# Fifteen small loads of 15 down to 1 partitions behind the first chunk of a softmax kernel

## The chip, the core and the metric

The kernel runs on one core of one Trainium2 chip. The metric is the device time of one execution in microseconds (us); less is better. A program on one core shows no second, slower state in these runs: all of them were of state fast, at a granted clock of 1.00. Each comparison was made on one chip, with runs of the kernel before in between.

## The reference

A softmax over the last axis of a float32 tensor of 16 x 256 x 32768, with temperature 1:

```python
scaled = logits / temperature
scaled = scaled - scaled.max(axis=-1, keepdims=True)
exp_scaled = np.exp(scaled)
return exp_scaled / exp_scaled.sum(axis=-1, keepdims=True)
```

It reads 536.87 MB and writes 536.87 MB. There is one exponential per element; the traffic to and from HBM (431 GB/s over the span of the kernel before) sets the scale, as the profile below shows.

## The kernel before

Each row of 32768 numbers is cut into two halves of 16384, which lie on two partitions. So there are 64 groups of 128 partitions, each of two chunks of 128 x 8192 numbers (4 MB, 32 KB a partition). A chunk is loaded into one of six buffers, worked on in place, and stored from the same buffer. VectorE takes the maximum, ScalarE the exponential; after both chunks of a group a few small instructions give the factor, and the two engines scale half of a chunk each. All loads and stores are issued from one queue, SyncE's, in program order:

```python
_BUFS = 6
_LAST_DMA = 4096

def load(i):                       # chunk i
    g, c = divmod(i, C)
    xs = xpool.tile([P, CW], fp32, tag="x", name="xs")
    slots[i] = xs
    for s, n in spans(CW, _LAST_DMA if g in (0, G - 1) else CW):   # first group: two halves
        tc.keep_in_program_order(
            nc.sync.dma_start(out=xs[:, s : s + n],
                              in_=x[g * P : (g + 1) * P, c * CW + s : c * CW + s + n]))

# ... store(), exps(), factors(), scales() cut ...

order = [("L", i) for i in range(min(_BUFS, n_chunks))] + [("S", 0)]
for i in range(1, n_chunks):
    order.append(("S", i))
    if i + _BUFS - 1 < n_chunks:
        order.append(("L", i + _BUFS - 1))
```

Six chunks are loaded at the start, as eight transfers, because the two chunks of the first group go in halves. From there on a store and a load alternate. In the text, 0a and 0b are the two halves of chunk 0, 1a and 1b those of chunk 1, L2 is the load of chunk 2, S0 the store of chunk 0.

## Time and profile before

| | before |
|---|---|
| median (lowest to highest) | 2494.44 us (2492.15 to 2495.24, 6 runs) |
| share of the chain of waits that is DMA | 96% |
| busy VectorE, ScalarE | 60%, 56% |
| rate from 500 to 2400 us | 433 GB/s |

These lines are from the page of the kernel before: the slices of the span (DMA is the mean busy share of the 16 DMA engines in tenths, GB/s what they moved), and the chain of work that ended last.

```profile
DMA  9999999999999999999999999999999999999998
GB/s 412 433 430 432 429 431 432 433 433 434 433 434 432 435 432 435 432 435 431 436 431 435 432 434 433 434 433 433 433 433 433 433 433 434 434 433 434 432 431 368
...
DMA 96%; SPq 1%; ACT 1%; DVE 1%; issue 1%; ACTq 0%
```

The DMA engines are busy for 90% or more of every slice but the last, and 96% of the chain runs through them. The rate is 433 GB/s from 500 us to 2400 us. Against that, only the first slice (412) and the last (368) leave something.

The next view is the table of stages: for each window, its length, the busy time of VectorE, ScalarE and GpSimd with their instruction counts, the clock, the mean busy share of the DMA engines and the rate in GB/s.

```profile
core 0: us, DVE busy (x) ACT busy (x) POOL busy (x), PEclk, DMA share, GB/s
6.00:12.00 6.00, 0.00 (x0) 0.00 (x0) 0.00 (x0) 1.00 1.01 434
12.00:18.00 6.00, 5.11 (x1) 1.28 (x1) 0.00 (x0) 1.00 1.02 437
18.00:24.00 6.00, 4.90 (x2) 2.39 (x1) 0.00 (x0) 1.00 1.02 437
...
125.00:500.00 375.00, 223.21 (x145) 210.89 (x69) 0.00 (x0) 1.00 1.00 431
500.00:2400.00 1900.00, 1138.55 (x735) 1072.70 (x344) 0.00 (x0) 1.00 1.00 433
2440.00:2500.00 60.00, 14.66 (x17) 15.47 (x9) 0.00 (x0) 1.00 0.74 318
```

From 6 us on the engines work without a break (DMA share 1.00 to 1.02) until the last 60 us. The rate is 2 GB/s lower up to 500 us than later.

The queue's own timeline shows how the opening loads are issued (start, length, what; consecutive issues are merged; SPq is SyncE's queue, L64 a line of the kernel), and VectorE's shows when the first two halves of the first group are there:

```profile
0.73 3.92 SPq L64 DMA_DIRECT2D xs<-in_logits_dram  x8
```

```profile
12.89 8.69 DVE L107 TENSOR_REDUCE nm<-xs 128x1 f32<-128x8192 f32 x1 [12.89 <-DMA xs<-in_logits_dram]
22.68 8.69 DVE L107 TENSOR_REDUCE nm<-xs 128x1 f32<-128x8192 f32 x1 [1.10 <-DMA xs<-in_logits_dram]
```

All eight opening loads are issued by 4.65 us, without a wait, so some 58 us of work lie before the DMA engines (the last of these loads landed at 62.21 us).

**Out of step, counted from the trace.** Two counts are in the trace but on no page.

The first is the spread of landing marks. Each transfer over 128 partitions left 16 marks on its semaphore, one by one: the first half of chunk 0, for one, from 7.55 to 7.93 us. There are 16 DMA engines, so the author takes each mark for the end of one engine's share, and the time from the first to the last of the 16 for how far apart the engines are; the trace does not name the engines. Before, it is 0.35 us for the opening loads, 0.60 us at 100 us, 2.0 at 200, 4.2 at 300, 6.5 at 500, then 7.1 at 1000, 8.5 at 1500, and 10.45 us for the last store. So, read this way, the engines do get out of step without help.

The second is the excess of long packets. Most packets of one 32 KB row took 1.213 us, those of a 16 KB row 0.611 us. What longer packets took beyond that is, summed over the 16 engines, 23.2 us up to 62 us, 2.5 us from 62 to 120 us, 26.8 us from 120 to 500 us, and 7.6 us in all the time after.

### The profile page before, as it was taken

The page shows a single profiled execution, that of the slowest core. Times are in us where ns is not written, and L with a number is a line of the kernel's source. Part 1 is how long each engine was busy: PE and PEld are TensorE (multiplying, and loading weights), DVE is VectorE, ACT ScalarE, POOL GpSimd, SP SyncE. Part 2 cuts the span into 40 slices and gives each one's busy share as a digit, 9 for nine tenths or more (in the row PEclk, how much of TensorE's full clock was granted, in tenths as well). Part 3 has the DMA queues.
Part 4 walks back from the last instruction along what each step waited for, and adds up shares of the span by engine and source line. Part 5 has one row for each costly group of instructions (what it writes and reads, how often), then busy time and mean ns, then how long its engine had stood idle before and what let it go on. Part 6 is the DMA issues. An engine that isn't in the chain of part 4 may idle for free.

```text
span 2493.8 us, 2234 instructions
## 1 busy us (share of the span) xinstructions
DVE 1487.4 (60%) x964; ACT 1405.0 (56%) x455; POOL 0.2 (0%) x4
## 2 busy tenths in 40 slices
DVE  7655565556655566555665566655666566655663
ACT  5665554655556555565555655555546555465553
POOL 0000000000000000000000000000000000000000
DMA  9999999999999999999999999999999999999998
GB/s 412 433 430 432 429 431 432 433 433 434 433 434 432 435 432 435 432 435 431 436 431 435 432 434 433 434 433 433 433 433 433 433 433 434 434 433 434 432 431 368
DMA packets 37745, 1073.90 MB, mean 431 GB/s; under 512 B 4192, under 2 KB 4192, under 8 KB 4192
## 3 DMA queue, kind: packets, MB, share of 16 engines
q1 hardware_dynamic: 37728, 1073.76, 99.9%
q14 instruction: 17, 0.14, 0.0%
HBM read 536.87 MB, written 536.87 MB: 431 GB/s over the span
## 4 chain that ended last, share of the span: by engine, by line
DMA 96%; SPq 1%; ACT 1%; DVE 1%; issue 1%; ACTq 0%
DMA out_dram<-xs 93%; DMA xs<-in_logits_dram 2%; SPq L64 1%; DVE nm L107 1%; ACT xs L163 1%; ACT xs L114 0%; ACTq L224 0%; SPq L75 0%; DVE f L150 0%; ACT ee L131 0%; DVE rS L149 0%; DVE Sh L87 0%; DVE ttj L138 0%; DVE Sh L84 0%; DVE Sh L138 0%
## 5 line engine op out<-in xcount | busy, mean ns | idle before, releaser
L114 ACT ACTIVATE xs<-xs,nm 128x8192 f32<-128x8192 f32 (+1 forms) x130 | 912.1, 7016 | 972.4 <-DVE nm L107 972.4
L107 DVE TENSOR_REDUCE nm<-xs 128x1 f32<-128x8192 f32 (+1 forms) x130 | 1111.6, 8551 | 527.3 <-DMA xs<-in_logits_dram 527.3
L163 ACT ACTIVATE xs<-xs,f 128x4096 f32<-128x4096 f32 (+1 forms) x130 | 468.1, 3648 | 71.4 <-DVE f L150 71.4
L160 DVE TENSOR_SCALAR xs<-xs,f 128x4096 f32<-128x4096 f32 (+1 forms) x130 | 295.7, 2318 | 3.7 <-DVE f L150 1.8
L138 DVE CUSTOM_DVE_ANT_0 ttj<-ee,ssum 128x2 f32<-128x2 f32 x64 | 10.3, 161 | 423.8 <-ACT ee L131 423.8
L114 ACT ACTIVATION_READ_ACCUMULATOR xs<-xs,nm 128x1 f32 x130 | 24.2, 186 | 0.0
L131 ACT ACTIVATE ee<-nm,nMh 128x2 f32<-128x2 f32 x64 | 17.9, 280 | 0.0
L150 DVE TENSOR_SCALAR f<-ee,rS 128x2 f32<-128x2 f32 x64 | 14.6, 229 | 2.2
L149 DVE RECIPROCAL rS<-Sh 128x1 f32<-128x1 f32 x64 | 10.5, 164 | 2.2
L87 DVE TENSOR_TENSOR nMh<-nMh 128x1 f32<-128x1 f32 x64 | 10.2, 160 | 2.2
L87 DVE TENSOR_TENSOR Sh<-Sh 128x1 f32<-128x1 f32 x64 | 10.2, 160 | 2.2
L129 DVE TENSOR_REDUCE nMh<-nm 128x1 f32<-128x2 f32 x64 | 9.9, 155 | 2.2
L84 DVE STREAM_SHUFFLE nMh<-nMh 128x1 f32<-128x1 f32 x64 | 9.7, 151 | 0.0
L84 DVE STREAM_SHUFFLE Sh<-Sh 128x1 f32<-128x1 f32 x64 | 9.7, 151 | 0.0
L114 ACT ACT_TABLE_LOAD x1 | 1.3, 1283 | 12.9 <-DMA xs<-in_logits_dram 12.9
L138 DVE DVE_READ_ACCUMULATOR2_ANT Sh<- 128x1 f32 x64 | 5.3, 84 | 0.0
L84 DVE LOAD_MASK_SELECT Sh<-Sh x64 | 0.9, 14 | 2.8
L84 DVE LOAD_MASK_SELECT nMh<-nMh x64 | 0.9, 14 | 2.7
L210 POOL MEMSET const-bfloat16-1.0<- 128x1 bf16 x1 | 0.1, 102 | 0.0
L210 POOL MEMSET const-uint8-127<- 128x1 uint8 x1 | 0.1, 102 | 0.0
L210 POOL MEMSET const-float32-0.0<- 128x1 f32 x1 | 0.1, 99 | 0.2 <-issue 0.2
L210 POOL MEMSET const-float32-1.0<- 128x1 f32 x1 | 0.1, 99 | 0.0
## 6 DMA issues: line engine op xcount, KB each, us to landing
out_dram<-xs SPq DMA_DIRECT2D x126, 4096.0 KB, 38.2
xs<-in_logits_dram SPq DMA_DIRECT2D x124, 4096.0 KB, 29.0
xs<-in_logits_dram SPq DMA_DIRECT2D x8, 2048.0 KB, 22.3
out_dram<-xs SPq DMA_DIRECT2D x4, 2048.0 KB, 26.7
```

Source lines behind the costliest of these rows:

```text
L64: nc.sync.dma_start(out=xs[:, s : s + n], in_=x[g * P : (g + 1) * P, c * CW + s : c * CW + s + n],)
L84: nc.vector.stream_shuffle(out=v[:, j + 1 : j + 2], in_=v[:, j : j + 1], mask=mask)
L87: nc.vector.tensor_tensor(out=v[:, j + 1 : j + 2], in0=v[:, j : j + 1], in1=v[:, j + 1 : j + 2], op=op,)
L107: nc.vector.tensor_reduce(out=nm[:, k : k + 1], in_=xs[:, s : s + n], axis=X, op=A.max, negate=True)
L114: nc.scalar.activation(out=xs[:, s : s + n], in_=xs[:, s : s + n], func=Exp, bias=nm[:, k : k + 1], scale=inv_t, accum_out=ssum[:, k : k + 1],
L129: nc.vector.tensor_reduce(out=nMh[:, 0:1], in_=nm, axis=X, op=A.min)
L131: nc.scalar.activation(out=ee, in_=nm, func=Exp, bias=nMh[:, n_rounds : n_rounds + 1], scale=-1.0,)
L138: nc.vector.tensor_tensor_reduce(out=ttj, in0=ee, in1=ssum, scale=1.0, scalar=0.0, op0=A.mult, op1=A.add, accum_out=Sh[:, 0:1],)
L149: nc.vector.reciprocal(out=rS, in_=Sh[:, n_rounds : n_rounds + 1])
L150: nc.vector.tensor_scalar_mul(out=f, in0=ee, scalar1=rS)
L160: nc.vector.tensor_scalar_mul(out=xs[:, s : s + cut], in0=xs[:, s : s + cut], scalar1=f[:, k : k + 1])
L163: nc.scalar.activation(out=xs[:, s + cut : s + n], in_=xs[:, s + cut : s + n], func=Copy, scale=f[:, k : k + 1],)
```

## The change

The intent: loads of 15, 14, ..., 1 partitions should give each engine one more small packet than the next, so that all engines are out of step from the start and the long packets are spared. The data go to the buffer of chunk 5, which is loaded over them later.

```diff
+_STAGGER = 512
@@ load
-        xs = xpool.tile([P, CW], fp32, tag="x", name="xs")
-        slots[i] = xs
+        if i not in slots:
+            slots[i] = xpool.tile([P, CW], fp32, tag="x", name="xs")
+        xs = slots[i]
@@
+    def stagger(i: int) -> None:
+        g, c = divmod(i, C)
+        slots[i] = xpool.tile([P, CW], fp32, tag="x", name="xs")
+        for n in range(15, 0, -1):
+            s = (n - 1) * _STAGGER
+            tc.keep_in_program_order(
+                nc.sync.dma_start(
+                    out=slots[i][:n, s : s + _STAGGER],
+                    in_=x[g * P : g * P + n, c * CW + s : c * CW + s + _STAGGER],
+                )
+            )
@@ main loop
             load(i)
             loaded = i + 1
+            if i == 0:
+                stagger(_BUFS - 1)
```

What the diff does not show is in the built program. The DMAs of SyncE's queue take turns on eight completion semaphores (99 to 103 and 105 to 107 in the trace after), and each waits for the one that last used its own: the 9-partition load was issued at 8.01 us, the last mark of 0a came at 7.99; the 8-partition load at 13.45 us, the last mark of 0b came at 13.43. The start of the queue, shortened (S0 to S7 here are the semaphores):

```
before                              after
0a 0b 1a 1b L2 L3 L4 L5   no waits  0a 0b  15x512 14x 13x 12x 11x 10x   no waits
                                     9x512   waits S0  (0a landed)
                                     8x512   waits S1  (0b landed)
                                     7x 6x 5x 4x 3x 2x 1x   wait S2 ... S7, S0
                                     1a      waits S1  (8x512 landed)
                                     1b L2 L3 L4 L5
```

## The prediction

> **What bounds the kernel now.** The DMA engines. The page puts 96% of the chain of waits on DMA; VectorE is busy 60%, ScalarE 56%. The slice row shows 430 to 435 GB/s in nearly every slice, first 412, last 368. [...]
>
> What being in step costs now can be read from the DMA packets. An undisturbed 32 KB packet takes 1.213 us. Those longer than that sum to about 55 us over 16 engines, nearly all in the first 500 us (430 to 431 GB/s there); after that almost none. In those 500 us the 16 landing marks of one transfer spread from 0.35 us apart to several us, and end 10.5 us apart: the engines get out of step by themselves, and the one held back most ends the kernel (354 GB/s from 2440 us on). All the change can win is a part of these 10 us, 0.4%.
>
> **What the change does.** It adds fifteen loads on the same queue, 0.24 MB, under 1 us of traffic. Intent: [...] about 0.08 us a step (2 KB at 27 GB/s, an estimate), 1.1 us from first to last. No run shows this yet.
>
> But the built order of the queue shows new waits. DMAs take turns on eight completion semaphores. Before, the eight opening loads use one each and are issued in 3.92 us without waiting (timeline). Now the two halves of chunk 0 and the 15-to-10-partition loads use all eight; the 9-partition load waits for the first half to land (7.9 us), the 8-partition load for the second (12.9 us, when VectorE starts), and load 1 comes only after eight more issues. At 0.49 us each (3.92/8) load 1 is issued near 16.8 us; its first packet follows 1.0 us later (as 0.73 to 1.75 us at the start): near 17.8 us. The engines would have gone on at 12.6 us. That is about 5.2 us idle, plus 0.3 to 0.6 us because the first packets after a standstill are slower (0.9 to 1.3 us instead of 0.61).
>
> Two consequences. The idle time is wholly on the critical path, since DMA work is continuous from there on. And all small loads have drained when load 1 starts, so the engines restart together and the stagger is lost: the early collisions stay about as they are.
>
> **Sum.** 2494.3 + 5.2 + 0.4 = about 2499.9 us; 8 in 10 between 2496 and 2503.5. Faster by over 2%: 0.5%; within 2%: 99%; slower by over 2%: 0.5%.
>
> **What would show it.** Second chunk's max starts on VectorE near 28 us instead of 22.7. The queue's own waits show the small loads waiting for logits loads. GB/s between 12 and 18 us falls to nearly none. First slice near 375 instead of 412. Landing marks of load 1 spread under about 0.5 us; still about 3 us collision excess per engine in the first 500 us; end spread again about 10 us. Steady rate 433. Compute durations unchanged.
>
> **What would make it wrong.** If the last small packets still leave engines offset when load 1 starts, collisions fall and up to 8 us comes back: 2492. If small loads issue more slowly than 0.49 us, or wait for each other's landing[...], the gap grows to 8 us or more. The lag of the slowest engine may also come out differently by chance: runs of before differ by 3 us.

The step of 0.08 us is an estimate from 433 GB/s over 16 engines; afterwards the 120 small packets took 0.084 us in the median. "Collisions" are a name for what packets took over the usual time (1.213 us for 32 KB); that engines meet anywhere is not shown.

## The result, and the profile after

| | before | after |
|---|---|---|
| median | 2494.44 us | 2500.97 us |
| lowest to highest, 6 runs each | 2492.15 to 2495.24 | 2500.33 to 2501.82 |
| ratio of the fast runs | | 1.0028 (95%: 1.0015 to 1.0041) |

Ratios here are the mean time of one kernel's fast runs over that of the other's of the same rounds, so not quite the ratio of the medians. The change costs 6.5 us by the medians: within 2%, but clear of the noise. The two profiled runs are only 5.15 us apart, as the profile of before was taken of its slowest run of the six (2495.24 us): what follows from the traces can be up to 0.8 us small.

The slices of the page after; the chain reads 96% DMA as before:

```profile
DMA  9999999999999999999999999999999999999998
GB/s 382 426 430 432 430 431 434 430 434 433 432 435 433 432 435 431 434 433 433 434 432 433 435 431 434 433 433 434 432 434 433 432 435 432 432 436 431 435 430 374
```

The first slice fell from 412 to 382 GB/s; the rest is as before. The same table of stages as above, after:

```profile
core 0: us, DVE busy (x) ACT busy (x) POOL busy (x), PEclk, DMA share, GB/s
6.00:12.00 6.00, 0.00 (x0) 0.00 (x0) 0.00 (x0) 1.00 1.01 431
12.00:18.00 6.00, 4.47 (x1) 1.28 (x1) 0.00 (x0) 1.00 0.37 85
18.00:24.00 6.00, 4.22 (x1) 1.75 (x1) 0.00 (x0) 1.00 0.98 415
...
125.00:500.00 375.00, 223.24 (x150) 212.01 (x68) 0.00 (x0) 1.00 1.00 431
500.00:2400.00 1900.00, 1137.60 (x736) 1074.20 (x343) 0.00 (x0) 1.00 1.00 433
2440.00:2500.00 60.00, 15.89 (x18) 19.61 (x13) 0.00 (x0) 1.00 0.84 359
```

From 12 to 18 us the rate fell from 437 to 85 GB/s. The rates from 125 to 500 us and from 500 to 2400 us are the same to the unit, so the stagger bought nothing there; the last row is higher only because the kernel ends later. (The stages between 24 and 125 us are left out: one short slow stretch, told of below under what stays open, falls on either side of their border.)

The queue's timeline after, and VectorE's first two maxima:

```profile
0.73 0.87 SPq L66 DMA_DIRECT2D xs<-in_logits_dram  x2
1.65 14.46 SPq L178 DMA_DIRECT2D xs<-in_logits_dram  x15
16.16 2.90 SPq L66 DMA_DIRECT2D xs<-in_logits_dram  x6
```

```profile
13.53 8.69 DVE L109 TENSOR_REDUCE nm<-xs 128x1 f32<-128x8192 f32 x1 [13.53 <-DMA xs<-in_logits_dram]
28.38 8.69 DVE L109 TENSOR_REDUCE nm<-xs 128x1 f32<-128x8192 f32 x1 [6.16 <-DMA xs<-in_logits_dram]
```

The fifteen loads hold the queue from 1.65 to 16.11 us, and load 1a is issued at 16.16 us, where before it was issued at 1.64 us. What held it is in the view of the queue's own waits (who waited for what: us in total, times, longest), in a line that the kernel before does not have:

```profile
SPq L178 <- DMA xs<-in_logits_dram: 9.2, 3, 5.2
```

9.2 us of waiting, in three waits, for loads to land. Waiting alone costs nothing here: while the 9-partition load waited for 0a, up to 8.01 us, the engines moved on at 431 GB/s (6 to 12 us). It costs once they have emptied what was queued. In the packets, the last of chunk 0 ended at 12.49 us and the first of chunk 1 began at 17.14 us: 4.65 us in which only small packets passed, the last of them until 16.97 us. Issuing alone would not have done it: the fifteen issues took 4.7 us in sum, so without waits load 1a would have been out near 7 us (an estimate), long before 12.49.

**The lag.** The simplest account of the loss is to ask at what time each kernel had moved a given amount of its real data (packets of 16 KB and more). The kernel after lags by 0.0 us at 4 MB, which is all of chunk 0; by 5.64 us at 5 MB; 5.66 at 12 MB; 6.0 at 100 MB; 5.8 at 800 MB; 5.7 at 1070 MB. The whole loss arises between 12 and 18 us, and nothing is won back in all that time. Only the last packet is less late, 4.7 us, as the engines end closer together in this run (last marks 9.25 us apart, before 10.45).

And the stagger? The landing marks of load 1a spread by 0.47 us after, 0.35 before; those of the transfers that land from 75 to 120 us by 0.5 to 1.1 us after, and 0.4 to 0.9 us before. The engines are about as much in step as they were.

### The profile page after: what moved, and what is told of

Read it like the earlier page. It is cut to its first block, busy times and chain, and to the rows that moved or that the text cites. A ratio compares the mean times of both kernels' runs of the same rounds, so it can differ in the third digit from the quotient of the medians.

```text
span 2498.6 us, 2252 instructions
## 1 busy us (share of the span) xinstructions
DVE 1487.4 (60%) x964; ACT 1405.0 (56%) x455; POOL 0.2 (0%) x4
## 4 chain that ended last, share of the span: by engine, by line
DMA 96%; SPq 1%; ACT 1%; DVE 1%; issue 1%; ACTq 0%
DMA out_dram<-xs 93%; DMA xs<-in_logits_dram 2%; SPq L66 1%; DVE nm L109 1%; ACT xs L165 1%; ACT xs L116 0%; SPq L178 0%; ACTq L240 0%; SPq L77 0%; DVE f L152 0%; ACT ee L133 0%; DVE rS L151 0%; DVE Sh L89 0%; DVE ttj L140 0%; DVE Sh L86 0%
## 5 line engine op out<-in xcount | busy, mean ns | idle before, releaser
L152 DVE TENSOR_SCALAR f<-ee,rS 128x2 f32<-128x2 f32 x64 | 14.6, 228 | 2.2
L151 DVE RECIPROCAL rS<-Sh 128x1 f32<-128x1 f32 x64 | 10.5, 164 | 2.2
```

The source lines that it names most:

```text
L151: nc.vector.reciprocal(out=rS, in_=Sh[:, n_rounds : n_rounds + 1])
L152: nc.vector.tensor_scalar_mul(out=f, in0=ee, scalar1=rS)
```

## The experiments

Theory A: the cost is idle time of the DMA engines, made by the turns on eight semaphores; and as the small loads have drained by then, the stagger is gone when load 1a starts. Rival B: being out of step is itself what costs. Rival C: the small loads' own work costs, by their number or bytes. A question beyond: had the stagger been kept, would it have paid?

Edits are shown against the changed kernel. All results were correct. The first four runs shared one set of runs of the kernel before (median 2494.64 us, 2493.56 to 2497.78, 11 runs).

### gap_only: the waits without the stagger

```diff
-                    out=slots[i][:n, s : s + _STAGGER],
-                    in_=x[g * P : g * P + n, ...],
+                    out=slots[i][:16, s : s + _STAGGER],
+                    in_=x[g * P : g * P + 16, ...],
```

> Fifteen loads of 16 partitions each instead of 15 down to 1[...]; the order of the queue and its waits stay. Theory A (the cost is the idle gap of the DMA engines, made by taking turns on eight completion semaphores): the gap stays, about 85 GB/s between 12 and 18 us, time about 2501 us, ratio to before 1.0020 to 1.0035. Rival B (being out of step is what costs): the cost goes, about 2494.5 us. Rival C (the small loads' own work costs): about 2501 us too, as A.

(The 0.16 us for 4 KB in the next two is twice the 0.08 us of the prediction, an estimate too.)

Measured: 2502.09 us (2501.94 to 2502.41), ratio 1.0029 (1.0017 to 1.0041). Its queue and its stage from 12 to 18 us:

```profile
1.64 15.87 SPq L178 DMA_DIRECT2D xs<-in_logits_dram  x15
17.55 2.95 SPq L66 DMA_DIRECT2D xs<-in_logits_dram  x6
```

```profile
12.00:18.00 6.00, 3.96 (x1) 1.28 (x1) 0.00 (x0) 1.00 0.35 76
```

With fifteen equal loads, meant to put no engine out of step, the cost is still there, so B falls. It is about 1 us above the changed kernel, which A accounts for: these issues are slower (about 0.42 us each against 0.25 to 0.29 for the waiting ones there), load 1a was issued at 17.55 instead of 16.16 us, and the lag at 5 MB was 7.15 us.

### six_loads: a stagger without the waits

```diff
-_STAGGER = 512
+_STAGGER = 1024
-        for n in range(15, 0, -1):
-            s = (n - 1) * _STAGGER
+        for m, n in enumerate((15, 12, 10, 7, 5, 2)):
+            s = m * _STAGGER
```

> Six loads of 15, 12, 10, 7, 5 and 2 partitions, 1024 numbers each, instead of fifteen: with the two halves of chunk 0 that is eight transfers, so none of the small ones waits, and load 1 waits only for the first half of chunk 0. The lead[...] is about as intended, 6 x 0.16 = 1.0 us. Theory A: no gap, over 400 GB/s between 12 and 18 us, and 2493 to 2495.5 us; if being out of step by 1 us also avoids the early collisions (long packets), as low as 2489 us. Rival B: about 2500 us. Rival C (cost per small load, 6.5 us / 15 = 0.43 us each): about 2497 us.

Measured: 2495.94 us (2495.74 to 2496.66), ratio 1.0005 (0.9993 to 1.0017). The queue's timeline shows that load 1a is issued at 8.01 us, when 0a has landed and 0b keeps the engines busy:

```profile
1.64 2.23 SPq L178 DMA_DIRECT2D xs<-in_logits_dram  x6
8.01 8.66 SPq L66 DMA_DIRECT2D xs<-in_logits_dram  x6
```

The stagger is kept this time: the marks of load 1a spread by 1.52 us. And it does not cost 5 us, so B falls again. But the time is not under before either; it lies just above the 2493 to 2495.5 us expected. And "over 400 GB/s between 12 and 18 us" missed: it was 289 GB/s, a lag of 2.4 us at 5 MB, at a DMA share of 1.02, at which the kernel before moved 437: the engines were busy, but the packets took longer.

```profile
12.00:18.00 6.00, 4.16 (x1) 1.28 (x1) 0.00 (x0) 1.00 1.02 289
```

The next run shows the small loads by themselves.

### six_even: neither stagger nor waits

```diff
-_STAGGER = 512
+_STAGGER = 1024
-        for n in range(15, 0, -1):
-            s = (n - 1) * _STAGGER
+        for m, n in enumerate((16,) * 6):
+            s = m * _STAGGER
```

(As above, `out` and `in_` over 16 partitions.)

> As six_loads, but all six loads have 16 partitions: no gap and no stagger, control for six_loads. Theory A: 2494.5 us plus 1.0 us of traffic[...], so about 2495.5 us; the difference to six_loads is what the stagger alone is worth. Rival B: about 2495 us, 5 us less than six_loads. Rival C: about 2497 us.

Measured: 2501.46 us, and unsteady (2497.89 to 2514.19, 6 runs), ratio 1.0033 (1.0014 to 1.0052). The expectation missed in two ways. The lag at 5 MB was 3.5 us, not 1.0: a 4 KB packet took 0.60 us (median 0.593), where 0.16 was expected. Sixteen engines at 4096 bytes in 0.60 us are 109 GB/s, and all six loads together, 0.39 MB from 11.99 to 15.59 us, give 109 GB/s too. Whether the number of the packets, their bytes or the few partitions that they go to make them slow, this run does not tell; the next one moves the same bytes to twice the partitions. Second, the profiled run ended with a spread of 15.6 us and had an excess of 14.6 us after 500 us, where the kernel before has 7.6; why this kernel varies so much from run to run is open. As a control for six_loads it is therefore worth little by its time. Its lag up to 100 MB (2.3 to 3.6 us) is usable.

### six_even32: the same bytes over twice the partitions

Against six_even: 512 numbers instead of 1024, and 32 partitions instead of 16.

```diff
-_STAGGER = 1024
+_STAGGER = 512
-        out=slots[i][:16, s : s + _STAGGER]
+        out=slots[i][:32, s : s + _STAGGER]
```

> As six_even (same bytes, same number of loads, no stagger, no gap), but each load spreads over 32 partitions of 512 numbers instead of 16 of 1024. In six_even a 4 KB packet took 0.60 us where 0.16 was expected: sixteen engines at 109 GB/s together. [...] a 2 KB packet takes about 0.15 us while all engines run small loads (0.30 us per load and engine), and the lag at 5 MB falls from 3.5 to about 1.7 us, 2495.5 to 2496.5 us. If small packets cost by their number or by being HBM reads: 0.30 us or more per 2 KB packet and a lag of 3.5 us or more.

(The 0.15 us is for a rate that doubles with the partitions, from the 109 GB/s of six_even.)

Measured, in the later set of runs (before 2494.05 us, 2492.04 to 2495.56, 9 runs): 2497.83 us (2496.91 to 2506.45, 4 runs), ratio 1.0023 (1.0008 to 1.0038). The lag at 5 MB fell from 3.46 to 1.90 us (expected 1.7). The same 0.39 MB took from 12.05 to 13.99 us, which is 203 GB/s, near twice 109. (A 2 KB packet took 0.11 us in the median.) So the small packets are held up by neither their number (twice as many here) nor their bytes (the same): the rate nearly doubled with the partitions. Why is not shown: the run reads twice as many rows of HBM as well, and no run changes one without the other. The times are above what was expected, and one of the four runs, 2506.45 us, is as far out as those of six_even; that stays open too.

### pool_queue: the same fifteen loads from another queue

```diff
-                nc.sync.dma_start(
+                nc.gpsimd.dma_start(
                     out=slots[i][:n, s : s + _STAGGER],
```

> The same fifteen loads of 15 down to 1 partitions, issued from GpSimd's queue, which has completion semaphores of its own: the opening loads no longer wait for them, except the load of chunk 5, which goes into the same buffer, while 40 us of transfers are still queued. Theory A: no gap, about 2494.5 us (2492 to 2496), perhaps lower if the engines stay out of step. Rival C: about 2501 us. [...]

(That the queue has semaphores of its own shows in the timeline below: seven loads of SyncE's queue issued in 3.42 us, none waiting for its turn.)

Measured: 2495.17 us (2495.01 to 2495.60), ratio 1.0002 (0.999 to 1.0014). SyncE's queue, and the stage:

```profile
0.74 3.42 SPq L66 DMA_DIRECT2D xs<-in_logits_dram  x7
```

```profile
12.00:18.00 6.00, 2.44 (x1) 1.28 (x1) 2.07 (x4) 1.00 1.00 390
```

All the fifteen loads, all their bytes, and the cost is gone from the time: C falls as the cause of the 6.5 us. The small loads are not free, though: this kernel lags by 1.7 us at 5 MB, 2.0 at 20 MB, 1.2 at 28 MB and 0.7 at 800 MB. About 0.9 us of what comes back is a slow stretch that this kernel does not have (see what stays open), so the time alone flatters it. The same holds for six_loads. In the built program seven opening loads no longer wait, and only L5, issued at 27.31 us, waits for the small ones. The stagger came out larger than intended, as the small packets spread over 19 us (5.4 to 24.8 us) between those of chunks 0 and 1: the marks of load 1b spread by 3.3 us, and by 3.0 at 100 us. Yet the kernel is not faster than before.

### eight_loads and thirty_loads: a shorter and a longer wait

```diff
 eight_loads
-        for n in range(15, 0, -1):
+        for n in range(15, 0, -2):

 thirty_loads: each load in two, the same bytes
-_STAGGER = 512
+_STAGGER = 256
-        for n in range(15, 0, -1):
-            s = (n - 1) * _STAGGER
+        for m in range(30):
+            n = 15 - m // 2
+            s = m * _STAGGER
```

> Eight loads of 15, 13, ..., 1 partitions, 512 numbers each: only the last two wait for the halves of chunk 0, and load 1 follows the last one directly. Theory A (the cost is the idle gap, and the gap is what is left to issue once the second half of chunk 0 has landed at 12.8 to 13.4 us): load 1 issued near 14.0 us instead of 16.16, so about 2.2 us of the lag of 5.6 us goes: a lag of about 3.4 us once 5 MB have moved, 2497.5 to 2498.5 us. A cost by number or bytes of the small loads: 8/15 or 64/120 of 6.5 us, about 2498 us too, so this run alone does not tell; thirty_loads does.

> Each of the fifteen loads cut into two of 256 numbers: the same bytes[...], the same intended stagger, twice the issues. Theory A: about 15 more issues of 0.3 us between the landing of chunk 0 and load 1, which is issued near 20.5 us instead of 16.16; lag 9.5 to 10.5 us, about 2505.3 us (2504 to 2507). If the bytes or the stagger cost: unchanged, about 2501 us.

Measured, with the same runs of before as six_even32: eight_loads 2498.57 us (2498.04 to 2500.26), ratio 1.0020 (1.0006 to 1.0034); thirty_loads 2505.84 us (2505.16 to 2506.67), ratio 1.0047 (1.0035 to 1.0060); the first is 0.07 us over its range, the second inside. The queue's timelines, first eight_loads, then thirty_loads:

```profile
1.65 12.03 SPq L178 DMA_DIRECT2D xs<-in_logits_dram  x8
13.90 2.89 SPq L66 DMA_DIRECT2D xs<-in_logits_dram  x6
```

```profile
1.64 19.38 SPq L179 DMA_DIRECT2D xs<-in_logits_dram  x30
21.07 2.92 SPq L66 DMA_DIRECT2D xs<-in_logits_dram  x6
```

The four kernels that make the engines wait, side by side. "Idle" is from the end of the last packet of chunk 0 to the start of the first of chunk 1; the lag is against before at 5 MB; "time" is what the medians show over before:

| | load 1a issued, us | idle, us | lag, us | lag - idle | time, us |
|---|---|---|---|---|---|
| eight_loads | 13.90 | 2.43 | 3.34 | 0.91 | 4.5 |
| changed kernel | 16.16 | 4.65 | 5.64 | 0.99 | 6.5 |
| gap_only | 17.55 | 6.09 | 7.15 | 1.06 | 7.5 |
| thirty_loads | 21.07 | 9.57 | 10.47 | 0.90 | 11.8 |

From the first row to the last, load 1a is issued 7.17 us later and the lag grows by 7.13 us. The lag follows the issue of load 1a (their difference is the same in all four rows within 0.2 us), whatever the number of loads, their bytes (the changed kernel and thirty_loads move the same) or their grading (gap_only has fifteen equal ones). That is theory A, shown. The time is 0.3 to 1.3 us more than the lag, part of which may be the slow run that was profiled of before. The constant 0.9 to 1.1 us is what a standstill costs besides: the first packets after it were slow (mostly 0.9 to 1.25 us instead of 0.61, as at the start of the kernel before: mostly 0.9 to 1.35).

### six_wide: a large stagger that is kept

Six loads as in six_loads, of 4096 numbers each, two in each of the buffers of chunks 3, 4 and 5.

```diff
-_STAGGER = 512
+_STAGGER = 4096
-        slots[i] = xpool.tile([P, CW], fp32, tag="x", name="xs")
-        for n in range(15, 0, -1):
-            s = (n - 1) * _STAGGER
+        for m, n in enumerate((15, 12, 10, 7, 5, 2)):
+            s = m % 2 * _STAGGER
+            if s == 0:
+                i = _BUFS - 3 + m // 2
+                g, c = divmod(i, C)
+                slots[i] = xpool.tile([P, CW], fp32, tag="x", name="xs")
```

> Six loads of 15 to 2 partitions as in six_loads, but 4096 numbers each and so 16 KB packets of 0.61 us or more: a stagger of 3.7 us or more without the long waits of the queue, as large as the 4 to 6 us to which the engines come by themselves in the first 500 us. Question: does a stagger of that size, really kept, save time? Theory A': no. Landing marks of load 1 spread by 3.5 us or more; excess of long packets from 120 to 500 us falls below 12 us (26.8 before), but the engine that was held back stays behind, the last spread is 10 us or more, and the lag at 5 MB (4 to 8 us, from 0.84 MB[...] at 109 GB/s) is not won back: 2497 to 2503 us. Rival: the stagger of the change was only too small; then the time falls below before, under 2492 us.

(The 109 GB/s is the rate of six_even.)

Measured: 2502.04 us (2501.75 to 2502.53), beside before 2494.44 us (2493.24 to 2495.12, 9 runs), ratio 1.0031 (1.0017 to 1.0045). The stages of six_wide, to be read against those of before above:

```profile
12.00:18.00 6.00, 3.96 (x1) 1.28 (x1) 0.00 (x0) 1.00 1.14 145
18.00:24.00 6.00, 4.73 (x1) 1.24 (x1) 0.00 (x0) 1.00 0.93 117
125.00:500.00 375.00, 227.97 (x150) 212.00 (x68) 0.00 (x0) 1.00 1.00 433
```

A stagger that is kept does spare the long packets: the marks of the load of 1a spread by 4.50 us, still 4.5 at 120 us, and the excess from 120 to 500 us fell from 26.8 to 1.5 us; the rate there is 433 GB/s from the start. (The kernels whose engines start in step have 15 to 29 us there, so 26.8 is one draw of several; six_loads and pool_queue, with smaller staggers, have 12.9 and 14.3, not clearly less.) But that is 25.3 us over 16 engines, 1.6 us of time, and the lag, with the 0.84 MB of the stagger's own 16 KB packets taken out, shows just that: 9.7 us at 40 MB, 8.2 at 400 MB, and 8.0 at 800 MB. Setting up such a stagger had cost 11.0 us by 12 MB (at 5 MB 10.6, or 5.4 with the stagger's packets counted; 4 to 8 was expected): from 18 to 24 us the rate was 117 GB/s, near the 109 of six_even. The last spread was 8.7 us, a little less than the "10 us or more" that was expected.

## Why the prediction was right

It foretold 2499.9 us and a range of 2496 to 2503.5; 2500.97 us came. Point by point:

- **The bound.** Right. The rates from 125 to 2400 us are the same to the unit, and the lag of 5.6 us stayed within half a microsecond up to 1070 MB: the idle time of the DMA engines at the start was not won back.
- **The mechanism.** Right: turns on eight semaphores, read from the built order of the queue. pool_queue keeps the fifteen loads and loses the waits, and the cost goes; gap_only keeps the waits and has equal loads, and the cost stays; four lengths of wait give four lags in step.
- **Its size.** Right in the sum, in part by luck: two errors went opposite ways. The eight issues from the 8-partition load to load 1a took 2.7 us, 0.34 us from one to the next, not 0.49. But the second half of chunk 0 was seen as landed at 13.44 us, not 12.9: its last mark came 0.65 us later than before, and the small loads were at work right behind it; that they caused the delay is likely, but was not tested by itself. Load 1a was issued at 16.16 us (predicted 16.8), idle was 4.65 us (5.2), the lag 5.64 us (5.2 plus 0.3 to 0.6).
- **The signs.** The second maximum started at 28.38 us (near 28). The first slice was 382 GB/s (near 375), and 12 to 18 us had 85 GB/s (nearly none: the stretch began with 0.5 us of chunk 0 and ended with 0.9 us of chunk 1). Load 1a's marks spread by 0.47 us (under 0.5). The excess up to 500 us was 63.9 us in all, 4.0 us per engine (about 3); the last spread 9.25 us (about 10).
- **What it overrated.** "Up to 8 us comes back" if the stagger survived. It was kept in three runs, at 1.5, 3 and 4.5 us, and none was faster than before. Only about 1.6 us of the time is lost to the long packets from 120 to 500 us, as six_wide shows by removing nearly all of their excess (26.8 to 1.5 us over 16 engines). The other part of the 10 us at the end does not come from the start. After 500 us the marks of before spread by a further 4.0 us (6.5 to 10.5), with little excess (7.6 us over 16 engines): 13 of the 14 packets over 60 ns late begin within 1 us of an instruction fetch on queue 14. There are 13 such fetches in that time, at 0.309 us or a little more each, 4.0 us together. That one engine carries all of them fits the growth of the spread, but is not shown: the trace does not name the engine.

Left open: a short stretch in which nearly all engines are slow together (58 to 62 us before, 64 to 68 us after; 14 and 20 us of excess, so 0.9 and 1.3 us of time). Where it occurs (before, after, gap_only, eight_loads, thirty_loads), it begins 2.6 us after the issue of the second store; in six_loads, six_even, six_even32, pool_queue and six_wide it is missing. Its cause was not sought. It matters for the comparisons: before has it, and so the kernels without it gain about 0.9 us that the account of waits and stagger does not explain. Of all kernels tried none beat the kernel before.

## What to carry to other kernels

Look at the built order of a queue with its semaphores before adding transfers to it: here, with eight completion semaphores taken in turn, the ninth transfer waited for the first to land (issued at 8.01 us, the first landed at 7.99), and a run of small ones behind a large one left the DMA engines nothing but small packets for 4.65 us before the next large one started. If such transfers are needed, put them on a queue with semaphores of its own (pool_queue: 2495.17 us), or keep them few enough to fit in the turns left (six_loads: 2495.94 us; the changed kernel 2500.97). And before spending anything on putting engines out of step, count what being in step costs, by summing the packets that took longer than the usual one and dividing by 16: here it was 1.7 us of 2494 (from 120 to 500 us).

## What the traces show besides

- The loads of 15 down to 1 partitions made 120 packets of 2 KB, and each load has n marks at landing and one at issue (at 2.24 us for the first, landed at 13.9 us). The engines of this all-DMA kernel start in step (marks 0.35 us apart) and come apart by themselves: 6.5 us at 500 us and 10.45 us at the end, with 26.8 us of excess of long packets from 120 to 500 us that a kept stagger of 4.5 us takes down to 1.5 us.
- Instruction fetches run beside the data: 8 KB packets on queue 14, 17 of them in the run before, 0.309 us each (one 0.318), each of the 13 after 500 us with a late data packet beside it.
- Small loads over 16 partitions (six_even) moved 109 GB/s together, over 32 partitions (six_even32) 203 GB/s.
- The time to issue a transfer depended on its partitions: on SyncE's queue (changed kernel, eight_loads, gap_only) 0.22 to 0.32 us for 1 to 9 partitions, 0.33 to 0.38 us for 10 to 14, 0.48 us for 15 (always the first small load), mostly 0.42 us for 16, and 0.33 to 0.53 us for 128.
